# Forming the first quarter of a feed-forward hidden layer from seven block products instead of eight

## The chip, the cores and the metric

The kernel runs on one core of a Trainium2 chip. The metric is device time in microseconds (us) of one execution. Five engines work side by side, each through its own list of instructions in order: TensorE (PE, matrix products), VectorE (DVE), ScalarE (ACT), GpSimd (POOL) and SyncE (SP). In this kernel SP starts the plain loads from HBM, and POOL starts the loads that add what they bring to what already lies in the buffer ("accumulating loads").

## The reference, cut to what matters

One layer of a decoder trunk over 512 tokens with model width 1024. The part that is changed is the first product of the feed-forward step, and the part that reads it is the second:

```
h = rmsnorm(x, g_mlp[i])
x = x + jnp.square(jax.nn.relu(h @ w_ff1[i])) @ w_ff2[i]
```

Here `h` is 512 x 1024, `w_ff1` is 1024 x 4096 and `w_ff2` is 4096 x 1024. Before it come two attentions with their gates and the product with `w_o`; behind it comes a gated embedding (`w_pe`, `w_pg`) and a final norm. All is float32.

## The kernel before

Every product runs in float32r, a form in which TensorE takes a rounded operand. To keep float32 accuracy each operand is split in two: `hi`, rounded by ACT (line 75), and `lo = x - hi`, by DVE (line 76). `split` does both. Each product then takes three matmuls (`mm3`, lines 93 to 95): hi·hi, hi·lo and lo·hi. Weights come from HBM as units of 128 x 1024 numbers (512 KB).

Activations stand with the model dimension on the 128 partitions: `h2` is eight tiles (`h2_0` to `h2_7`) of 128 x 512 tokens, each as a pair hi and lo. They are made by `turned`: TensorE transposes the residual `x2` into a PSUM bank, and ACT and DVE split it from there with the gain as scale. The norm's factor is applied later (`rr`).

The feed-forward runs over four kilocolumns q (1024 of the 4096 hidden columns each). For each, eight blocks m of 128 columns are formed by `columns` (24 matmuls with 512 token columns each, PSUM tile `f{q}_{m}`), then relu and square give `u`. The second product over one kilocolumn, `products(q)`, already uses a scheme of seven block products for a 2 x 2 partition (Winograd's form): its steps are p1, p7, p6, p4, p5, p2, p3, with the PSUM tiles `pc`, `pb`, `pa`. Where such a product needs sums of weight blocks, the sum is formed in the buffer by accumulating loads (`more`, on POOL): the buffer `tx` is first loaded with one block and given a second (for p7), then a third (for p6), then a fourth (for p4). Each addition must wait until ACT and DVE have split the sum before it. `products` is a generator; the loop over q advances it between the blocks m of the next kilocolumn, so that TensorE alternates between the two.

The order of the instructions on each engine is fixed when the program is built, by a scheduler with a timeline of its own; on the chip each engine follows its list and waits wherever an operand isn't there. Buffers go round in pools: `fpool`'s tag `raw` has 8 buffers of 512 KB, and a load into a buffer waits for the last reader of what was there.

Of the kernel before, what the change touches and what calls it, by code (L numbers as in the profile page):

```python
# [11 lines left out]
F32 = mybir.dt.float32  # L12
# [28 lines left out]
def trunk(ctx, tc, xT_in, x_in, pT_in, w_in, w_up_a, w_up_b, w_o, w_ff1, w_ff2, w_pe, w_pg, g_final, pack, scratch, out):  # L41
# [119 lines left out]
    def gcol(i, k):  # L161
        return pk[:, 8 * i + k:8 * i + k + 1]
# [332 lines left out]
    def plain(name):  # L495
        return fpool.tile([P, U], F32, tag="raw", name=name, bufs=8)

    def factor(name):
        return [fpool.tile([P, U], F32R, tag=f"m{e}", name=f"m{e}{name}", bufs=2) for e in ("hi", "lo")]

# [27 lines left out]

    x2 = [[slot(f"x2_{t}{j}", "x") for j in range(2)] for t in range(NT)]

    def turned(name, dst, i, k, tag):
        ps = bank(f"{name}p{k}", tag)
        for t in range(NT):
            nc.tensor.transpose(ps[:, t * P:(t + 1) * P], x2[t][k // 4][:, k % 4 * P:(k % 4 + 1) * P], ident)
        split(*dst[k], ps, gcol(i, k))

    def squares(name, ss, j, t):
        nc.scalar.activation(half(f"{name}{j}{t}", "e", 3), x2[t][j], AF.Square, accum_out=ss[j][:, t:t + 1])


    h2 = [pair(f"h2_{k}", "h") for k in range(KD)]
    ss = [small(f"ss2_{j}", 4) for j in range(2)]
    for j in range(2):
        for t in range(NT):
            nc.sync.dma_start(x2[t][j], x_in[t * P:(t + 1) * P, j * S:(j + 1) * S])
        ps = [bank(f"wo{j}_{t}", (("p", "p", "p", "z"), ("at", "at", "o", "z"))[j][t]) for t in range(NT)]
        for c in range(4):
            whi, wlo = unit(w_o[4 * j + c], S)
            for k in range(2):
                hi, lo = merged[2 * c + k]  # L550
                for t in range(NT):
                    cols = slice(t * P, (t + 1) * P)
                    mm3(ps[t], hi[:, cols], lo[:, cols], whi[:, k], wlo[:, k], c == 0 and k == 0, c == 3 and k == 1)
            if j == 1 and c == 1:
                for k in range(4):
                    turned("h2", h2, 1, k, ("p", "p", "p", "z")[k])
        for t in range(NT):
            nc.vector.tensor_tensor(x2[t][j], x2[t][j], ps[t], op=ALU.add)
            squares("junk", ss, j, t)
    for _ in embed(0, ("p", "p", "p", "z")):  # L560
        pass
    for k in range(4, KD):
        turned("h2", h2, 1, k, ("at", "at", "o", "z")[k - 4])


    nc.vector.tensor_tensor(ss[0], ss[0], ss[1], op=ALU.add)
# [4 lines left out]

    tt = nc.vector.tensor_tensor

    def products(q, ua, ub):
        a11, a21 = [ua[:, :, i * 256:(i + 1) * 256] for i in range(2)]
        a12, a22 = [ub[:, :, i * 256:(i + 1) * 256] for i in range(2)]

        def load(name, kh, jh):  # L580
            t = [plain(f"{name}_{q}{c}") for c in range(2)]
            for c in range(2):
                nc.sync.dma_start(t[c], w_ff2[((q * 2 + kh) * 2 + jh) * 2 + c])
            return t

        def more(t, kh, jh):
            for c in range(2):
                nc.gpsimd.dma_start(t[c], w_ff2[((q * 2 + kh) * 2 + jh) * 2 + c], accum_op=ALU.add)  # L588

        def area(name, tag):  # L590
            return [bank(f"{name}{q}_{i}", tag) for i in range(2)]

        def product(name, a, b, ps, start=False, g=None, then=None):
            m = [x.rearrange("p (k c) -> p k c", k=4) for x in factor(f"{name}{q}")]
            w = []
            if not callable(a):
                split(*m, a, g)
            for c in range(2):
                count[0] += 1
                pool, n = ((wpool, 3), (fpool, 2))[c]  # L600
                w.append([pool.tile([P, U], F32R, tag=f"w{e}", name=f"w{e}{count[0]}", bufs=n) for e in ("hi", "lo")])
                split(*w[c], b[c])
            if callable(a):
                for h in range(2):
                    split(*[x[:, 2 * h:2 * h + 2] for x in m], a(h), g)
            for c in range(2):
                whi, wlo = [x.rearrange("p (k c) -> p k c", k=2) for x in w[c]]
# [12 lines left out]

        def mixed(name):
            return fpool.tile([P, U], F32, tag="s", name=f"{name}_{q}", bufs=2).rearrange("p (k c) -> p k c", k=4)

        def mix(name, x, y):
            s = mixed(name)
# [12 lines left out]
        ty = tx  # L638
        if q == 3:
            more(tx, 1, 0)  # L640
            ty = load("ty", 0, 1)
            more(ty, 1, 1)
            more(ty, 0, 0)
        t1, b21, b22 = load("t1", 0, 1), load("b21", 1, 0), load("b22", 1, 1)
        more(t1, 0, 0)
        yield
        ss = []

        def sums(h):
            if h == 0:  # L650
                ss.extend([mixed(f"s{i}") for i in (1, 2)])
# [12 lines left out]
        onto(pc, 1, 0)  # L664
        yield
        product("p5", s1, t1, pc, g=-1.0)
        onto(pb, 1, 0)
        yield
        pa = area("pa", "z")
        product("p2", a12, b21, pa, True)  # L670
        onto(pc, 1, 1)
        yield
        nc.vector.scalar_tensor_tensor(s2, a12, -1.0, s2, op0=ALU.mult, op1=ALU.subtract)

        def rest():
            onto(pa, 0, 0)
            if q == 3:
                first()

        product("p3", s2, b22, pc, then=rest)  # L680
        onto(pc, 0, 1)
        yield
# [8 lines left out]
                wg.append(unit(w_pg[k // 2], S))  # L691
            turned("h3", h3, 2, k, ("p", "p", "p", "o")[k])

    last = None
    for q in range(4):
        uu = [big(f"u{q}{i}", i, F32).rearrange("p (k c) -> p k c", k=4) for i in range(2)]
        this = products(q, *uu)
        for m in range(8):
            ps = bank(f"f{q}_{m}")
            columns(ps, unit(w_ff1[8 * q + m], P), h2)  # L700
            u = uu[m // 4][:, m % 4]
            nc.scalar.activation(u, ps, AF.Relu)
# [141 lines left out]
def _layout(x, p, w_in, w_up_a, w_up_b, w_o, w_ff1, w_ff2, w_pe, w_pg, g_mix, g_mlp, g_pe, g_final, sinks, rel_bias):  # L844
    pack = np.zeros((P, 168), np.float32)
    for i, g in enumerate((g_mix, g_mlp, g_pe)):
# [20 lines left out]
        "w_ff1": np.stack([_units(w_ff1, P * m, P) for m in range(DFF // P)]),  # L867
# [25 lines left out]
```

## Time and profile before

| | |
|---|---|
| median of 3 runs | 735.11 us (734.38 to 735.52) |
| the profiled execution | 733.58 us |
| its span, first to last instruction | 731.9 us |
| TensorE busy | 720.1 us, 98% of the span |
| VectorE, ScalarE busy | 501.2 us, 368.7 us |
| share of TensorE in the chain of work that ended last | 96% |

The span is what the profile's rows lie in; 1.7 us of the execution's own time lies around it. The rows give start times in us from the start of the span. A matmul's duration in the rows includes its way through the array (0.39 us for 512 columns), and the next one starts long before that has passed; what one costs is the distance between starts.

### The profile page before, as it was taken

To read this page: it belongs to the slowest core of one execution; us is meant where nothing else is said; L and a number is where in the kernel's file an instruction comes from. 1 tells how busy PE (TensorE), PEld (TensorE's weight loads), DVE (VectorE), ACT (ScalarE), POOL (GpSimd) and SP (SyncE) were. 2 spreads that over 40 slices of the span, in tenths; PEclk is the share of its full clock that TensorE was granted. 3 is DMA by queue.
4 is the path that set the end of the run, shared out by engine and by line. 5 is a ranking of instruction groups with operands and counts; after the bars stand their busy time and mean duration, and the time that the engine had idled before them with its cause. 6 is when DMAs were issued, how large, how long until landed. Compare 5 with 4: busy or idle time off the path is not lost.

```text
span 731.9 us, 9201 instructions
## 1 busy us (share of the span) xinstructions
PE 720.1 (98%) x3460; PEld 605.0 (83%) x3460; DVE 501.2 (68%) x731; ACT 368.7 (50%) x606; POOL 59.2 (8%) x84
## 2 busy tenths in 40 slices
PE   8999999999999999999999999999999999999995
PEld 7899888888888888888888888888888888888884
DVE  5695895898886548455275766666665765578586
ACT  7268978766544434345343433444434434245642
POOL 2010000211111000100000010101010011100000
PEclk9999999999999999999999999999999999999998
DMA  8331222122212225993235494647756589920202
GB/s 315 121 116 59 87 87 86 58 87 91 83 59 87 87 86 187 324 286 123 87 106 152 129 229 163 146 141 201 201 144 145 142 232 220 219 51 29 87 21 94
DMA packets 29227, 98.21 MB, mean 134 GB/s; under 512 B 3432, under 2 KB 3432, under 8 KB 29184
## 3 DMA queue, kind: packets, MB, share of 16 engines
q1 hardware_dynamic: 23040, 76.82, 30.5%
q0 software_dynamic: 5568, 20.01, 15.2%
q10 hardware_dynamic: 576, 0.80, 0.3%
q8 instruction: 27, 0.44, 0.2%
q14 instruction: 16, 0.13, 0.1%
HBM read 95.51 MB, written 2.11 MB: 133 GB/s over the span
## 4 chain that ended last, share of the span: by engine, by line
PE 96%; DVE 2%; ACT 1%; DMA 1%; issue 0%; SPq 0%; ACTq 0%
PE f L95 8%; PE f L94 8%; PE f L93 8%; PE pc L94 4%; PE pc L95 4%; PE pc L93 4%; PE bg L93 2%; PE bg L94 2%; PE ag L95 2%; PE bg L95 2%; PE ag L94 2%; PE ag L93 2%; PE wo L93 2%; PE wo L94 2%; PE pb L94 2%; PE pb L95 2%
## 5 line engine op out<-in xcount | busy, mean ns | idle before, releaser
L76 DVE TENSOR_TENSOR wlo<-wr,whi 128x1024 fp32r<-128x1024 f32 x86 | 105.1, 1223 | 78.8 <-ACT whi L75 78.3
L75 ACT CAST whi<-wr 128x1024 fp32r<-128x1024 f32 x86 | 90.2, 1052 | 135.7 <-PE f L94 30.5
L76 DVE TENSOR_TENSOR wlo<-b,whi 128x1024 fp32r<-128x1024 f32 x24 | 29.2, 1222 | 33.7 <-ACT whi L75 33.7
L94 PE MATMUL pc<-wlo,mhip 128*128 128x512 f32 x128 | 49.9, 390 | 0.0
L93 PE MATMUL pc<-whi,mhip 128*128 128x512 f32 x128 | 49.9, 390 | 0.0
L95 PE MATMUL pc<-whi,mlop 128*128 128x512 f32 x128 | 49.3, 389 | 0.0
L588 POOL DMA_DIRECT2D tx<-in_w_ff x24 | 20.8, 879 | 336.4 <-DVE wlo L76 162.6
L75 ACT CAST whi<-b 128x1024 fp32r<-128x1024 f32 x24 | 25.0, 1050 | 36.8 <-PE f L94 24.5
L76 DVE TENSOR_TENSOR wlo<-tx,whi 128x1024 fp32r<-128x1024 f32 x22 | 26.8, 1221 | 16.6 <-ACT whi L75 16.2
L75 ACT CAST whi<-tx 128x1024 fp32r<-128x1024 f32 x22 | 23.1, 1054 | 24.7 <-PE f L94 11.7
L413 DVE TENSOR_TENSOR_SCAN keep<-keep 128x128 f32<-128x128 f32 (+3 forms) x32 | 26.3, 860 | 3.8 <-POOL keep L408 1.9
L94 PEld LDWEIGHTS pc<-wlo,mhip 128*128 128x128 f32 x128 | 24.0, 188 | 5.2 <-DVE wlo L76 0.3
L93 PEld LDWEIGHTS pc<-whi,mhip 128*128 128x128 f32 x128 | 24.0, 188 | 5.0
L95 PEld LDWEIGHTS pc<-whi,mlop 128*128 128x128 f32 x128 | 24.0, 188 | 4.9
L75 ACT CAST mhip<-s 128x1024 fp32r<-128x1024 f32 (+1 forms) x16 | 13.4, 839 | 24.0 <-PE pc L94 12.8
L618 DVE SCALAR_TENSOR_TENSOR x<-pc,rr,x 128x512 f32<-128x512 f32 x32 | 22.6, 745 | 4.2 <-PE pc L95 4.2
L93 PE MATMUL wo<-whi,mg 128*128 128x512 f32 x64 | 25.0, 390 | 0.0
L94 PE MATMUL wo<-wlo,mg 128*128 128x512 f32 x64 | 24.9, 389 | 0.0
L93 PE MATMUL pb<-whi,mhip 128*128 128x512 f32 x64 | 24.9, 389 | 0.0
L94 PE MATMUL pb<-wlo,mhip 128*128 128x512 f32 x64 | 24.9, 389 | 0.0
L95 PE MATMUL pb<-whi,mlop 128*128 128x512 f32 x64 | 24.9, 389 | 0.0
L95 PE MATMUL wo<-whi,mg 128*128 128x512 f32 x64 | 24.7, 389 | 0.0
(987 smaller groups left out, 2122.6 us busy)
## 6 DMA issues: line engine op xcount, KB each, us to landing
wr<-in_w_in SPq DMA_DIRECT2D x32, 512.0 KB, 3.3
wr<-in_w_ff SPq DMA_DIRECT2D x32, 512.0 KB, 3.3
b<-in_w_ff SPq DMA_DIRECT2D x24, 512.0 KB, 4.6
tx<-in_w_ff POOLq DMA_DIRECT2D x24, 512.0 KB, 5.7
wr<-in_w_o SPq DMA_DIRECT2D x8, 512.0 KB, 3.9
tx<-in_w_ff SPq DMA_DIRECT2D x8, 512.0 KB, 3.2
t<-in_w_ff SPq DMA_DIRECT2D x8, 512.0 KB, 6.1
t<-in_w_ff POOLq DMA_DIRECT2D x8, 512.0 KB, 10.3
```

The costliest lines, as they stand in the source:

```text
L75: nc.scalar.copy(hi, src)
L76: nc.vector.tensor_tensor(lo, src, f32(hi), op=ALU.subtract)
L93: nc.tensor.matmul(ps, ahi, bhi, start=start, stop=False, skip_group_check=more)
L94: nc.tensor.matmul(ps, ahi, blo, start=False, stop=False, skip_group_check=more)
L95: nc.tensor.matmul(ps, alo, bhi, start=False, stop=stop, skip_group_check=more)
L413: nc.vector.tensor_tensor_scan(rev, rev, rev, 1.0, op0=ALU.mult, op1=ALU.min)
L588: nc.gpsimd.dma_start(t[c], w_ff2[((q * 2 + kh) * 2 + jh) * 2 + c], accum_op=ALU.add)
L618: nc.vector.scalar_tensor_tensor(x2[2 * i + t][j], ps[t], rr[j][:, 2 * i + t:2 * i + t + 1], x2[2 * i + t][j], op0=ALU.mult, op1=ALU.add)
```

## The change

The first kilocolumn (q = 0) of `h @ w_ff1` is no longer formed by eight `columns` blocks but by a new generator `hidden`, in seven block products over halves of the tokens (i), of the model rows (kh) and of the kilocolumn (jh). Each has four 128-column parts m, four 128-row parts k and 256 tokens: 48 matmuls with 256 columns. In the order of the program they are f1, f7, f6, f4, f5, f2, f3. They sum up in the PSUM tiles `fc` (f1, f6, f5, f3), `fb` (f7, f4) and `fa` (f2). `keep` copies a partial sum to `u`, `done` adds one to `u` and applies relu and square.

```diff
+    def blocks(src, q):
+        def load(name, kh, jh):
+            t = [plain(f"{name}_{q}{c}") for c in range(2)]
+            for c in range(2):
+                nc.sync.dma_start(t[c], block(c, kh, jh))
+            return t
+
+        def more(t, kh, jh):
+            for c in range(2):
+                nc.gpsimd.dma_start(t[c], block(c, kh, jh), accum_op=ALU.add)
...
-        split(*dst[k], ps, gcol(i, k))
+        if whole is None:
+            split(*dst[k], ps, gcol(i, k))
+        else:
+            nc.scalar.activation(whole, ps, AF.Copy, scale=gcol(i, k))
+            split(*dst[k], whole)
...
+    hf = [plain(f"hf{i}").rearrange("p (k c) -> p k c", k=2) for i in range(4)]
...
+            if j == 1 and c == 0:
+                f11, fx = fetch("f11", 0, 0), fetch("fx", 0, 1)
+                add(fx, 1, 1)
...
+    def hidden(ua, ub):
...
+        def product(name, a, b, ps, start=False, g=None):
+            w = halves(b)
+            if len(a) != 4:
+                m = [x.rearrange("p (k c) -> p k c", k=4) for x in factor(name)]
+                split(*m, a[0], g)
+                a = [[x[:, k] for x in m] for k in range(4)]
+            for m in range(4):
+                dst = ps[m // 2][:, m % 2 * 256:(m % 2 + 1) * 256]
+                for k in range(4):
+                    whi, wlo = [x[:, k % 2, m * P:(m + 1) * P] for x in w[k // 2]]
+                    mm3(dst, whi, wlo, *a[k], start and k == 0 and m % 2 == 0, k == 3, True)
...
+        chain, side = area("fc", "at"), area("fb", "z")
+        product("f1", known(0, 0), f11, chain, True)
+        s3 = mix(mixed("fs3"), rows(0, 0), rows(1, 0))
+        product("f7", [s3], fx, side, True)
+        keep(chain, 0, 0)
+        add(fx, 0, 0)
+        s1 = mix(mixed("fs1"), rows(1, 0), rows(1, 1))
+        s2 = mix(mixed("fs2"), s1, rows(0, 0))
+        f1 = fetch("f1", 0, 1)
+        add(f1, 0, 0)
+        yield
+        product("f6", [s2], fx, chain)
+        keep(side, 1, 1)
...
+        add(fx, 1, 0)
+        f21, f22 = fetch("f21", 1, 0), fetch("f22", 1, 1)
+        product("f4", known(1, 1), fx, side)
+        keep(chain, 1, 0)
+        product("f5", [s1], f1, chain, g=-1.0)
+        done(side, 1, 0)
+        yield
+        side = area("fa", "z")
+        product("f2", known(0, 1), f21, side, True)
+        done(chain, 1, 1)
+        product("f3", [s2], f22, chain)
+        done(side, 0, 0)
...
-    last = None
-    for q in range(4):
-        uu = [big(f"u{q}{i}", i, F32).rearrange("p (k c) -> p k c", k=4) for i in range(2)]
+    uu = kilo(0)
+    last = products(0, *uu)
+    sevens = hidden(*uu)
+    next(sevens)
+    next(sevens)
+    next(last)
+    next(sevens)
+    for q in range(1, 4):
+        uu = kilo(q)
         this = products(q, *uu)
...
-            if last and m < 5:
+            left = 8 - q
+            if m < left:
                 next(last)
-            if m in (3, 5, 6):
+            if m == left - 2:
+                next(this)
+            if left <= m < 7 + (q < 3):
                 next(this)
```

The unsplit `h2` is now kept in four buffers `hf` of the tag `raw`, since the sums s1, s2, s3 are made of it. The sums of weight blocks come from accumulating loads into `fx` (two halves, `fx_00` and `fx_01`: two blocks for f7, a third for f6, a fourth for f4) and into `f1` (two blocks, for f5).

On TensorE the rows behind the last transposes of `h2` were blocks `f0_m` with 512 columns. Before, they begin so:

```order
L534 MATMUL h2p7_3317<-ident_80,x2_31_2927 128x128
L93 MATMUL f0_0_3348<-h2_0h_2928,whi50_3351 128x512
L94 MATMUL f0_0_3348<-h2_0l_2929,whi50_3351 128x512
L95 MATMUL f0_0_3348<-h2_0h_2928,wlo50_3352 128x512
L93 MATMUL f0_0_3348<-h2_1h_2930,whi50_3351 128x512
```

Now the seven products stand there one behind the other, 336 matmuls, with no block of another kilocolumn between them. Where f6 ends (`fc1`, weights 55) and f4 begins (`fb0`, weights 56 and 57, the two halves of the last `fx`), the rows are:

```order
L95 MATMUL fc1_3371<-mhif6_3517,wlo55_3514 128x256
L93 MATMUL fb0_3372<-h2_4h_2936,whi56_3583 128x256
L94 MATMUL fb0_3372<-h2_4l_2937,whi56_3583 128x256
L95 MATMUL fb0_3372<-h2_4h_2936,wlo56_3584 128x256
L93 MATMUL fb0_3372<-h2_5h_2938,whi56_3583 128x256
L94 MATMUL fb0_3372<-h2_5l_2939,whi56_3583 128x256
L95 MATMUL fb0_3372<-h2_5h_2938,wlo56_3584 128x256
L93 MATMUL fb0_3372<-h2_6h_2940,whi57_3587 128x256
L94 MATMUL fb0_3372<-h2_6l_2941,whi57_3587 128x256
```

The seventh matmul of f4 is the first that needs `whi57`, the rounded second half of `fx` with its fourth block in it.

POOL's accumulating loads of the first kilocolumn were these before, all for `products(0)`:

```order
L588 DMA tx_00_3484<-in_w_ff2 128x1024
L588 DMA tx_01_3485<-in_w_ff2 128x1024
L588 DMA t1_00_3671<-in_w_ff2 128x1024
L588 DMA t1_01_3672<-in_w_ff2 128x1024
L588 DMA tx_01_3485<-in_w_ff2 128x1024
L588 DMA tx_00_3484<-in_w_ff2 128x1024
```

Now eight for `hidden` stand ahead of those (x2 is two equal rows in succession):

```order
L510 DMA fx_00_3132<-in_w_ff1 128x1024
L510 DMA fx_01_3133<-in_w_ff1 128x1024 x2
L510 DMA fx_00_3132<-in_w_ff1 128x1024 x2
L510 DMA f1_00_3503<-in_w_ff1 128x1024
L510 DMA f1_01_3504<-in_w_ff1 128x1024
L510 DMA fx_01_3133<-in_w_ff1 128x1024
L510 DMA tx_00_3709<-in_w_ff2 128x1024
```

So the last addition to `fx_01` stands behind the last one to `fx_00` and both of `f1`. SP's loads in the same stretch, which before were units of `w_ff1` in the order of m, are now:

```order
L87 DMA wr73_4090<-in_w_ff1 128x1024
L505 DMA f1_00_3503<-in_w_ff1 128x1024
L505 DMA f1_01_3504<-in_w_ff1 128x1024
L505 DMA f21_00_3575<-in_w_ff1 128x1024
L505 DMA f21_01_3576<-in_w_ff1 128x1024
L505 DMA f22_00_3579<-in_w_ff1 128x1024
L505 DMA f22_01_3580<-in_w_ff1 128x1024
L505 DMA b11_00_3705<-in_w_ff2 128x1024
```

The two of `f21` take over the buffers of `hf0` and `hf1`, which the sum s2 reads last; `f22_00` takes that of `fx_00` once it is split for f4, and `f22_01` and `b11_00` those of `hf2` and `hf3`.

## Rows read from the trace of the kernel before

**Rows 1.** The page: the chain that ended last, shares by engine

```profile
PE 96%; DVE 2%; ACT 1%; DMA 1%; issue 0%; SPq 0%; ACTq 0%
```

**Rows 2.** The longest waits of TensorE: for whom, us in total, times, longest

```profile
PE warm L150 <- DVE ones L144: 1.1, 1, 1.1
PE vb L93 <- ACT kvwhi L75: 1.1, 1, 1.1
...
```

**Rows 3.** TensorE in order of time, first kilocolumn: start, us, line; 20 rows

```profile
349.78 0.39 PE L95 MATMUL f<-h_4h,wlo 128*128 128x512 f32 x1
...
354.09 0.39 PE L94 MATMUL f<-h_7l,whi 128*128 128x512 f32 x1
```

**Rows 4.** The same with 256 columns, in the attention's values: 27 rows

```profile
42.88 0.28 PE L94 MATMUL va<-wlo,h_0h 128*128 128x256 f32 x1
...
45.99 0.28 PE L93 MATMUL va<-whi,h_1h 128*128 128x256 f32 x1
```

**Rows 5.** Busy us of PE, PEld, DVE, ACT, POOL; clock; DMA, by stretch

```profile
360.00:380.00 20.00, 20.00 (x90) 16.57 (x89) 12.02 (x13) 8.84 (x11) 0.85 (x1) 1.00 0.23 79
```

**Rows 6.** The turn from `w_o` to the first kilocolumn: DVE, then PE

```profile
337.30 1.23 DVE L76 TENSOR_TENSOR wlo<-wr,whi 128x1024 fp32r<-128x1024 f32 x1 [0.44 <-ACT whi L75]
344.32 0.74 DVE L79 SCALAR_TENSOR_TENSOR h_4l<-h2p,pk,h_4h 128x512 fp32r<-128x512 f32 x1
344.98 0.74 DVE L79 SCALAR_TENSOR_TENSOR h_5l<-h2p,pk,h_5h 128x512 fp32r<-128x512 f32 x1
...
341.41 1.91 PE L534 MATMUL h2p<-ident,x 128*128 128x128 f32 x16
343.08 0.47 PE L93 MATMUL f<-h_0h,whi 128*128 128x512 f32 x1
```

**Rows 7.** The page's costliest groups: the two halves of one split

```profile
L75 ACT CAST whi<-tx 128x1024 fp32r<-128x1024 f32 x22 | 23.1, 1054 | 24.7 <-PE f L94 11.7
L76 DVE TENSOR_TENSOR wlo<-tx,whi 128x1024 fp32r<-128x1024 f32 x22 | 26.8, 1221 | 16.6 <-ACT whi L75 16.2
```

**Rows 8.** From a finished split to the addition: DVE, then POOL

```profile
458.51 1.23 DVE L76 TENSOR_TENSOR wlo<-tx,whi 128x1024 fp32r<-128x1024 f32 x1 [3.08 <-ACT whi L75]
...
460.09 0.86 POOL L588 DMA_DIRECT2D tx<-in_w_ff  x1 [3.44 <-DVE wlo L76]
```

**Rows 9.** Three accumulating loads issued singly, 378.6 to 392.4: issue to landing

```profile
DMA to landing us min/median/max: 5.3/5.3/5.4
```

**Rows 10.** POOL in order of time, four accumulating loads close together

```profile
612.40 0.86 POOL L588 DMA_DIRECT2D ty<-in_w_ff  x1 [8.74 <-DMA ty<-in_w_ff]
612.99 2.05 POOL L588 DMA_DIRECT2D t<-in_w_ff  x2
618.99 0.86 POOL L588 DMA_DIRECT2D tx<-in_w_ff  x1 [3.95 <-DVE wlo L76]
```

**Rows 11.** Issue to landing of the fourth of them (618.99)

```profile
DMA to landing us min/median/max: 10.6/10.6/10.6
```

**Rows 12.** SP's plain loads around those four, and the landing of the later one

```profile
607.77 4.67 SPq L583 DMA_DIRECT2D b<-in_w_ff  x2
615.07 0.33 SPq L87 DMA_DIRECT2D wr<-in_w_pg  x1
...
DMA to landing us min/median/max: 9.8/9.8/9.8
```

**Rows 13.** The page: queues (q1 plain loads, q0 POOL's): packets, MB, share

```profile
q1 hardware_dynamic: 23040, 76.82, 30.5%
q0 software_dynamic: 5568, 20.01, 15.2%
```

**Rows 14.** TensorE's last matmul, and the stretches behind it (columns as rows 5)

```profile
722.49 0.28 PE L95 MATMUL pg<-wpg,h_7l 128*128 128x256 f32 x1
...
724.00:726.00 2.00, 0.00 (x0) 0.00 (x0) 1.83 (x9) 0.13 (x2) 0.00 (x0) 0.88 0.68 262
726.00:728.00 2.00, 0.00 (x0) 0.00 (x0) 1.71 (x6) 0.72 (x1) 0.00 (x0) 0.50 0.00 0
```

More of the change, by code (lines that the diff above doesn't have):

```diff
@@ L496, in plain, with block, halves, mixed @@
         return fpool.tile([P, U], F32, tag="raw", name=name, bufs=8)
+    def blocks(src, q):
+        def block(c, kh, jh):
+            return src[((q * 2 + kh) * 2 + jh) * 2 + c]
+        def load(name, kh, jh):
[6 more added lines that the diff above has]
+                nc.gpsimd.dma_start(t[c], block(c, kh, jh), accum_op=ALU.add)
+        return load, more
+    def halves(b):
+        w = []
+        for c in range(2):
+            count[0] += 1
+            pool, n = ((wpool, 3), (fpool, 2))[c]
+            w.append([pool.tile([P, U], F32R, tag=f"w{e}", name=f"w{e}{count[0]}", bufs=n) for e in ("hi", "lo")])
+            split(*w[c], b[c])
+        return [[x.rearrange("p (k c) -> p k c", k=2) for x in y] for y in w]
+    def mixed(name):
+        return fpool.tile([P, U], F32, tag="s", name=name, bufs=2).rearrange("p (k c) -> p k c", k=4)
     def factor(name):
@@ L529, in trunk, with turned @@
     x2 = [[slot(f"x2_{t}{j}", "x") for j in range(2)] for t in range(NT)]
-    def turned(name, dst, i, k, tag):
+    def turned(name, dst, i, k, tag, whole=None):
         ps = bank(f"{name}p{k}", tag)
@@ L541, in trunk @@
     h2 = [pair(f"h2_{k}", "h") for k in range(KD)]
+    hf = [plain(f"hf{i}").rearrange("p (k c) -> p k c", k=2) for i in range(4)]
     ss = [small(f"ss2_{j}", 4) for j in range(2)]
+    tt = nc.vector.tensor_tensor
+    fetch, add = blocks(w_ff1, 0)
     for j in range(2):
@@ L553, in trunk @@
                     mm3(ps[t], hi[:, cols], lo[:, cols], whi[:, k], wlo[:, k], c == 0 and k == 0, c == 3 and k == 1)
+            if j == 1 and c == 0:
+                f11, fx = fetch("f11", 0, 0), fetch("fx", 0, 1)
+                add(fx, 1, 1)
             if j == 1 and c == 1:
                 for k in range(4):
-                    turned("h2", h2, 1, k, ("p", "p", "p", "z")[k])
+                    turned("h2", h2, 1, k, ("p", "p", "p", "z")[k], hf[k // 2][:, k % 2])
         for t in range(NT):
@@ L562, in trunk @@
     for k in range(4, KD):
-        turned("h2", h2, 1, k, ("at", "at", "o", "z")[k - 4])
+        turned("h2", h2, 1, k, ("o", "p", "p", "p")[k - 4], hf[k // 2][:, k % 2])
     nc.vector.tensor_tensor(ss[0], ss[0], ss[1], op=ALU.add)
@@ L570, in trunk, with rows, known, area @@
     nc.vector.tensor_scalar(rr[1], rr[0], -1.0, None, op0=ALU.mult)
-    tt = nc.vector.tensor_tensor
+    def hidden(ua, ub):
+        u = [[x[:, :, i * 256:(i + 1) * 256] for x in (ua, ub)] for i in range(2)]
+        def rows(i, kh):
+            return [hf[2 * kh + c][:, :, i * 256:(i + 1) * 256] for c in range(2)]
+        def known(i, kh):
+            return [[x[:, i * 256:(i + 1) * 256] for x in h2[4 * kh + k]] for k in range(4)]
+        def area(name, tag):
+            return [bank(f"{name}{i}", tag) for i in range(2)]
+        def product(name, a, b, ps, start=False, g=None):
[9 more added lines that the diff above has]
+                    mm3(dst, whi, wlo, *a[k], start and k == 0 and m % 2 == 0, k == 3, True)
+        def mix(s, x, y):
+            for c in range(2):
+                xc, yc = [z[c] if isinstance(z, list) else z[:, 2 * c:2 * c + 2] for z in (x, y)]
+                tt(s[:, 2 * c:2 * c + 2], xc, yc, op=ALU.subtract)
+            return s
+        def parts(ps, i, j):
+            return [(u[i][j][:, 2 * b:2 * b + 2], ps[b].rearrange("p (m c) -> p m c", m=2)) for b in range(2)]
+        def keep(ps, i, j):
+            for dst, src in parts(ps, i, j):
+                nc.scalar.copy(dst, src)
+        def done(ps, i, j):
+            for dst, src in parts(ps, i, j):
+                tt(dst, dst, src, op=ALU.add)
+            full = u[i][j]
+            nc.scalar.activation(full, full, AF.Relu, scale=(1.0, -1.0)[j])
+            nc.scalar.activation(full, full, AF.Square)
+        chain, side = area("fc", "at"), area("fb", "z")
[11 more added lines that the diff above has]
+        keep(side, 1, 1)
+        for c in range(2):
+            nc.vector.scalar_tensor_tensor(s2[:, 2 * c:2 * c + 2], rows(0, 1)[c], -1.0, s2[:, 2 * c:2 * c + 2],
+                                           op0=ALU.mult, op1=ALU.subtract)
+        add(fx, 1, 0)
[10 more added lines that the diff above has]
+        done(side, 0, 0)
+        for dst, src in parts(chain, 0, 1):
+            nc.scalar.activation(dst, src, AF.Relu, scale=-1.0)
+        nc.scalar.activation(u[0][1], u[0][1], AF.Square)
+        yield
@@ L578, in products @@
         a12, a22 = [ub[:, :, i * 256:(i + 1) * 256] for i in range(2)]
[L580 to L588, printed above, removed]
+        load, more = blocks(w_ff2, q)
         def area(name, tag):
@@ L594, in product @@
             m = [x.rearrange("p (k c) -> p k c", k=4) for x in factor(f"{name}{q}")]
-            w = []
             if not callable(a):
                 split(*m, a, g)
[L598 to L602, printed above, removed]
+            w = halves(b)
             if callable(a):
@@ L606, in product @@
             for c in range(2):
-                whi, wlo = [x.rearrange("p (k c) -> p k c", k=2) for x in w[c]]
+                whi, wlo = w[c]
                 for k in range(2):
@@ L619, in onto @@
                                                x2[2 * i + t][j], op0=ALU.mult, op1=ALU.add)
-        def mixed(name):
-            return fpool.tile([P, U], F32, tag="s", name=f"{name}_{q}", bufs=2).rearrange("p (k c) -> p k c", k=4)
         def mix(name, x, y):
-            s = mixed(name)
+            s = mixed(f"{name}_{q}")
             tt(s, x, y, op=ALU.subtract)
@@ L650, in sums @@
             if h == 0:
-                ss.extend([mixed(f"s{i}") for i in (1, 2)])
+                ss.extend([mixed(f"s{i}_{q}") for i in (1, 2)])
             ks = slice(2 * h, 2 * h + 2)
@@ L692, in first, with kilo @@
             turned("h3", h3, 2, k, ("p", "p", "p", "o")[k])
-    last = None
-    for q in range(4):
-        uu = [big(f"u{q}{i}", i, F32).rearrange("p (k c) -> p k c", k=4) for i in range(2)]
+    def kilo(q):
+        return [big(f"u{q}{i}", i, F32).rearrange("p (k c) -> p k c", k=4) for i in range(2)]
+    uu = kilo(0)
[7 more added lines that the diff above has]
+        uu = kilo(q)
         this = products(q, *uu)
@@ L866, in _layout @@
         "w_o": np.stack([_units(w_o, S * j, S, 2 * c, 2) for j in range(2) for c in range(4)]),
-        "w_ff1": np.stack([_units(w_ff1, P * m, P) for m in range(DFF // P)]),
+        "w_ff1": np.stack([_units(w_ff1, S * j, S, 4 * k + 2 * c, 2) for k in range(2) for j in range(2) for c in range(2)]
+                          + [_units(w_ff1, P * m, P) for m in range(8, DFF // P)]),
         "w_ff2": np.stack([_units(w_ff2, S * j, S, 8 * q + 4 * k + 2 * c, 2)
```

## The prediction

> **What bounds the kernel now.** I read the chain of work that ended last first: TensorE holds 96% of it [rows 1]. Then TensorE's waits: the two longest are 1.1 us each and lie at the start of the program [rows 2]. So TensorE is the bound, and in the first kilocolumn nothing else shows: in the stretch 360 to 380 it is busy for all 20 us at full clock, while DVE is busy for 12.02 and ACT for 8.84 [rows 5]. There a change gains what it takes off TensorE, as long as it leaves no new hole in TensorE's row. Both are to be worked out.
>
> **What the change takes off TensorE.** Before, the first kilocolumn is 8 blocks of 24 matmuls with 512 columns, 192 in all. From 349.78 to 354.09 lie 19 distances between starts: 4.31 / 19 = 0.2268 us each [rows 3]. Now it is 7 products of 48 matmuls with 256 columns, 336. Matmuls of that shape stand in the values of the attention: 42.88 to 45.99, 26 distances, 3.11 / 26 = 0.1196 us [rows 4]; the weights are 128 x 128 there as here, so that their loading is hidden as well as it will be here. 192 x 0.2268 = 43.5 us against 336 x 0.1196 = 40.2 us: **-3.4 us**. The columns fall by an eighth, the time only by 7.7%, because a short matmul costs a little more than half a long one. The 16 transposes stay.
>
> **What it adds on ACT and DVE.** DVE gets in the 40 us of the seven products, counted from its order, 14 subtractions of 128 x 1024 (1.22 us each [rows 7]) and 16 of half that size (0.66 us apart, 344.32 to 344.98 [rows 6]): 17.1 + 10.6 = 27.7 us of 40. ACT gets less, since its cast is 1.05 us [rows 7], with one more short pass for each tile of `h2` (`hf`). Neither becomes the bound, and I cost their work at nothing by itself; TensorE's matmuls cover it, 5.7 us a product (48 x 0.1196). What counts is the chain through `fx`.
>
> **The chain through fx.** In the list of TensorE f1, f7, f6 and f4 follow each other without a filler; f7, f6 and f4 all use the one buffer `fx`, and between two uses lie a split, an addition from HBM and a split. I lay it out.
> - The last transposes start at 341.41 and the first matmul behind them at 343.08 [rows 6]; ahead of that point TensorE has the same work in both kernels. Without a wait f1, f7 and f6 take 144 matmuls, and the seventh of f4, the first to need `whi57`, would start at 343.08 + 150 x 0.1196 = 361.0.
> - `wlo52`, the split of `fx_00` for f7, stands in DVE's list where a weight's split stands before, behind the last sums with `w_o`: it ends at 337.30 + 1.23 = 338.5 [rows 6]. From such an end to the addition's issue are 460.09 - 459.74 = 0.35 us [rows 8]: 338.9. The loads that are free by then were issued long before, so this one runs alone: 5.3 us [rows 9], landed at 344.2. ACT 1.05 and DVE 1.22 [rows 7], and 0.1 for hand-over: split by 346.6. f6 is due at 343.08 + 96 x 0.1196 = 354.6; until then DVE has eight half-size steps (the sums s1 and s2, the lo parts of `h2`) and two splits left for it, 8 x 0.66 + 2 x 1.22 = 7.7 us, to 354.3: it just fits, no wait.
> - At 346.95 POOL issues the third addition to `fx_00`, and behind it, about 1 us apart, the two for `f1`. The third addition to `fx_01` must wait for `wlo55`, in DVE's list behind eight half-size steps: 346.6 + 8 x 0.66 + 1.22 + 0.35 = 353.4. So four accumulating loads leave POOL at about 0, 1, 2 and 6.5 us.
> - Alone the last one would land at 353.4 + 5.3 = 358.7, in time. But the trace has this very pattern: 612.40, 612.99 (two), 618.99 [rows 10], that is 0 to 2.6 and 6.6 us, and there the fourth lands 10.6 us after its issue, at 629.6 [rows 11]. The work explains it. On the page POOL's queue takes 15.2% of 731.9 us for 20.01 MB, 2.9 us of all 16 engines for 0.52 MB, and a plain load 1.5 us (30.5%, 76.82 MB) [rows 13]: four additions are 11.6 us, and the two plain loads in that stretch (612.1 and 615.07 [rows 12]) 3.0 us.
> - Here the plain loads in the same window are `f21_00`, `f21_01`, `f22_00`, `f22_01`, `b11_00`: five. How many get through before the fourth addition is not known. The load of 615.07 needed 9.8 us beside the additions [rows 12], so plain loads are held up as well. Lower bound, none: 346.95 + 5.3 + 3 x 2.9 = 361.0. Upper, all five: 353.4 + 10.6 + 3 x 1.5 = 368.5. I take three, one more than in the row: 353.4 + 10.6 + 1.5 = **365.5**.
> - `whi57` is cast at 365.5 + 0.1 + 1.05 = 366.7. TensorE stands from 361.0 to 366.7: **+5.7 us** (+1.2 and +8.7 at the bounds). Behind the waiting matmul stand the rest of f4, then f5, f2, f3: all of them shift, and nothing gives it back, since DVE, ACT and the loads of `f21` and `f22` were waiting on the same transfers. `wlo57` comes 1.22 us later, after eleven matmuls that don't need it (1.3 us).
>
> On such a queue the Trainium skill ("DMA: Bandwidth & Descriptors", Queues, rings and completion order) says that each DMA engine takes turns between the queues it has work for. By that rule all five plain loads would be served while the additions wait, and the sum would be its upper bound. The 9.8 us of [rows 12] agree with taking turns only in part, as more additions than loads went through.
>
> **The clock.** Five us without a matmul are new in this kernel's middle. At the end of the program the last matmul starts at 722.49, the granted clock is 0.88 as a mean of 724 to 726 and 0.50 after it [rows 14], that is 1.2 GHz: it fell some 3 us behind the last matmul. So I expect it to fall in the hole. What the return costs no row shows: nothing at the least, and at the most f4's remaining 42 matmuls at twice 0.1196, 5.0 us. I take a third, **+1.5 us**, since the return is likely done within f4.
>
> **Behind it.** In the second product p1 needs `u`, ready after f2, and f3 and one block of 5.4 us (24 x 0.2268) stand between. From q = 0 to 2 only one block stands between p7 and p6 (two before): 2 x 5.4 = 10.9 us from start to start, against 0.35 + 5.3 + 0.1 + 1.05 + 1.22 = 8.0 for addition and split; p6 to p4 has just that distance before and waits for nothing [rows 2]. I cost both at nothing; if that cover were gone, 8.0 us less what lies between would show as a wait of `pc`. The tail of the program is the same list.
>
> **Sum.** -3.4 + 5.7 + 1.5 = **+3.8 us**: 733.6 becomes 737.4 for the profiled execution. The median of the runs lies 1.5 us higher (735.11), so the predicted time is **738.9 us**.
>
> **The rivals.**
> - *The additions don't hold each other up*, `fx_01` lands by 359.9 (361.0 - 1.1) and the full gain stays: 735.1 - 3.4 = 731.7. For it speaks that an addition alone takes 5.3 us [rows 9], which would do; against it the 10.6 us of [rows 11]. It decides at a landing of 359.9, 13 us behind the first of four additions, which is nearly what they take without a plain load. Chance of this and of a gain over 0.2%: 0.19. The Trainium skill ("DMA: Bandwidth & Descriptors", Anatomy of one DMA) gives such a load about 2.0 us and the bytes at 436 GB/s, an estimate of 3.2 us for 0.52 MB; by that rule this rival would hold with time to spare. The trace disagrees: 5.3 us at the least.
> - *The hole eats just the gain.* The landing is 361.7 to 364.7, as at two plain loads or fewer: -3.4 + 2 to 5 us, and the clock hardly falls. 735 us, within 0.2% (1.5 us, about what a measurement of this kernel can tell from no change). Chance 0.18.
> - *f6 waits too.* If the second addition to `fx_00` lands not after 5.3 but, as beside other traffic, after up to 10.6 us [rows 11], the split ends 5.3 us later, f6 starts some 5 us late and the next additions move by as much: up to 743. For it speaks that f6 just fits; against it that SP has nothing to load just then. Chance 0.08.
> - *DVE becomes the bound*: 27.7 of 40 us, no; 0.02, some 740.
>
> **Chances and range.** The forecast itself (738.9, its own range 736.6 to 742.5) gets 0.53. Slower by over 0.2% is this and the last two: 0.63. The range reaches down to the lower bound of the transfers (735.1 - 3.4 + 1.2 = 732.9, and a little of the measurement's spread), up to five loads with a third of the clock's bound (735.1 - 3.4 + 8.7 + 1.5 = 741.9): **732.4 to 742.3**; the full gain without a hole and a late f6 stay outside.
>
> **What would show it.** In the profile after: distances of 0.1196 us in `fc`, `fb`, `fa`; a wait of TensorE for ACT's cast of `fx` (`fb<-h_6h,whi`), 3 to 8 us, and no other new one over 1 us; behind it a stretch with a granted clock of 0.5; four landings on POOL's queue of 5 to 12 us. Wrong it would be if POOL's last addition to `fx` lands within 6 us of its issue, if TensorE's hole stands at f6, or if the short matmuls start further apart than 0.12 us because their weights can't be loaded in time.

## The result and the profile after

The changed kernel takes 738.86 us (median of 5 runs, 737.24 to 741.25), the kernel before 735.11 us: a ratio of 1.0060, with a 95% interval of 1.0044 to 1.0076 (a ratio is formed from all runs and can differ by 0.1% from that of the medians). It is slower by 0.6%, and the forecast was 738.9 us. The profiled execution took 737.24 us and its span is 735.5 us, against 731.9 us before.

From the page of the changed kernel, POOL's DMA queue (packets, MB, share of 16 engines) and the shares of the chain that ended last:

```profile
q0 software_dynamic: 6720, 24.21, 18.9%
...
PE 91%; DVE 3%; DMA 3%; ACT 1%; issue 0%; SPq 0%; ACTq 0%
```

TensorE's share of the chain falls from 96% [rows 1] to 91%, and the 3% of DMA (22 us) say that the chain now runs through transfers somewhere. POOL's queue takes 18.9% of 735.5 us for 46 loads of 0.52 MB (24.21 MB), 3.0 us each of all 16 engines, about as before (2.9 [rows 13]). The waits of TensorE (whom it waited for, us in total, times, longest) say where:

```profile
PE fb L93 <- ACT whi L75: 4.5, 1, 4.5
PE vb L93 <- ACT kvwhi L75: 1.4, 1, 1.4
```

One new wait stands above those of [rows 2], of the product f4 (`fb`) for ACT's cast of a weight. TensorE's rows in order of time around it, with the first rows of f7, f6 and f4 ahead:

```profile
349.20 0.28 PE L93 MATMUL fb<-mhif,whi 128*128 128x256 f32 x1
...
354.96 0.40 PE L93 MATMUL fc<-mhif,whi 128*128 128x256 f32 x2
...
360.72 0.28 PE L93 MATMUL fb<-h_4h,whi 128*128 128x256 f32 x1
...
361.32 0.28 PE L95 MATMUL fb<-h_5h,wlo 128*128 128x256 f32 x1
366.11 0.58 PE L93 MATMUL fb<-h_6h,whi 128*128 128x256 f32 x1 [4.52 <-ACT whi L75]
366.49 0.42 PE L94 MATMUL fb<-h_6l,whi 128*128 128x256 f32 x1
...
370.55 0.31 PE L95 MATMUL fb<-h_5h,wlo 128*128 128x256 f32 x1
```

Three things stand here. From 349.20 to 360.72 are f7 and f6, 96 matmuls in 11.52 us, 0.1200 us each, so the short matmuls cost what [rows 4] said. The seventh matmul of f4 was due at 361.32 + 0.12 = 361.44 and starts at 366.11, a hole of 4.67 us. Behind it, from 366.49 to 370.55, lie 19 distances in 4.06 us, 0.214 each; at 0.12 they would be 2.28, so this stretch loses 1.8 us, and with the first, slow distance (0.38 for 0.12) 2.0 us. The busy times by stretch (PE, PEld, DVE, ACT, POOL, then TensorE's granted clock, the DMA share and GB/s), which answer to [rows 5], name the reason:

```profile
360.00:365.00 5.00, 1.59 (x14) 1.39 (x12) 0.85 (x1) 0.00 (x0) 0.00 (x0) 0.88 1.03 311
365.00:370.00 5.00, 3.89 (x18) 3.89 (x19) 3.69 (x4) 4.85 (x6) 0.00 (x0) 0.50 0.85 327
```

The granted clock falls within the hole and is 0.50 (1.2 GHz) from 365 to 370. DVE and ACT are nearly idle in the hole (0.85 us and nothing in 360 to 365): they wait as well. Only the DMA engines are full. POOL's issues in order of time:

```profile
339.15 0.86 POOL L510 DMA_DIRECT2D fx<-in_w_ff  x1 [21.41 <-DVE ss L605]
347.34 0.85 POOL L510 DMA_DIRECT2D fx<-in_w_ff  x1 [7.33 <-DVE wlo L76]
348.01 1.95 POOL L510 DMA_DIRECT2D f<-in_w_ff  x2
353.30 0.86 POOL L510 DMA_DIRECT2D fx<-in_w_ff  x1 [3.35 <-DVE wlo L76]
```

ACT's row with the cast that ends TensorE's wait, and that waits for the transfer itself:

```profile
365.02 1.04 ACT L75 CAST whi<-fx 128x1024 fp32r<-128x1024 f32 x1 [5.43 <-DMA fx<-in_w_ff]
```

The DMA view of the stretch lists the issues (tile, engine, count, KB each, median us from issue to landing); the first row is that of 347.34, the second the two for `f1`, the third that of 353.30:

```profile
fx<-in_w_ff POOLq DMA_DIRECT2D x1, 512.0 KB, 5.2
f<-in_w_ff POOLq DMA_DIRECT2D x2, 512.0 KB, 10.8
...
fx<-in_w_ff POOLq DMA_DIRECT2D x1, 512.0 KB, 11.7
```

The last addition lands 11.7 us after its issue, at 365.0, where that of 347.34, with no other addition ahead of it, needs 5.2.

From the issue of 347.34 to that landing at 365.02 the DMA view has for the two queues (packets, MB, share of 16 engines):

```profile
q0 software_dynamic: 576, 2.10, 64.2%
q1 hardware_dynamic: 551, 2.05, 30.7%
```

In these 17.7 us POOL's queue moved just the four additions (2.10 MB are 4 x 0.52) in 11.3 us of all engines, and the plain loads 2.05 MB, as much as 3.9 of them, in 5.4 us. Together that is 95% of the stretch: the engines were at work for nearly all the time that the addition was on its way.

The account of the two spans: -3.2 us for the columns (336 x 0.1200 = 40.3 for 43.5), +4.7 the hole, +2.0 the clock, +0.3 the longer wait of `vb` at the start of the program, and -0.1 behind TensorE's last matmul (9.2 us from its start at 726.26 to the end of the span, 9.4 before [rows 14]). Together +3.7 us with these rounded terms, and 735.5 - 731.9 is 3.6.

### The profile page after: what moved, and what is told of

Same layout as the page of the kernel before. It is cut to its first block, busy times and chain, and to the rows that moved or that the text cites. A ratio compares the mean times of both kernels' runs of the same rounds, so it can differ in the third digit from the quotient of the medians.

```text
span 735.5 us, 9559 instructions
## 1 busy us (share of the span) xinstructions
PE 719.1 (98%) x3604; PEld 611.3 (83%) x3604; DVE 514.5 (70%) x747; ACT 388.2 (53%) x631; POOL 66.1 (9%) x92
## 3 DMA queue, kind: packets, MB, share of 16 engines
q0 software_dynamic: 6720, 24.21, 18.9%
## 4 chain that ended last, share of the span: by engine, by line
PE 91%; DVE 3%; DMA 3%; ACT 1%; issue 0%; SPq 0%; ACTq 0%
PE f L94 6%; PE f L93 6%; PE f L95 6%; PE pc L94 4%; PE pc L93 4%; PE pc L95 4%; DMA fx<-in_w_ff 2%; PE bg L93 2%; PE bg L94 2%; PE ag L95 2%; PE bg L95 2%; PE ag L94 2%; PE ag L93 2%; PE pb L93 2%; PE pb L94 2%; PE pb L95 2%
## 5 line engine op out<-in xcount | busy, mean ns | idle before, releaser
L75 ACT CAST whi<-wr 128x1024 fp32r<-128x1024 f32 x78 | 81.7, 1051 | 101.9 <-PE ag L94 18.2
L76 DVE TENSOR_TENSOR wlo<-wr,whi 128x1024 fp32r<-128x1024 f32 x78 | 95.2, 1221 | 42.9 <-ACT whi L75 42.5
L76 DVE TENSOR_TENSOR wlo<-b,whi 128x1024 fp32r<-128x1024 f32 x24 | 29.0, 1221 | 27.7 <-ACT whi L75 27.7
```

## The experiments

All ratios are to the kernel before, run beside each experiment on the same chip. The theory under test: the addition is late because the additions issued ahead of it on POOL's queue are served first, and because plain loads come between; its delay is TensorE's hole; and the hole makes the clock fall. The rivals are that only the plain loads hold it up, that additions in flight share the engines, and that the slow stretch behind the hole is not the clock's.

### The last addition ahead of the two for f1

```diff
         f1 = fetch("f1", 0, 1)
-        add(f1, 0, 0)
         yield
         product("f6", [s2], fx, chain)
...
         add(fx, 1, 0)
+        add(f1, 0, 0)
...
+    with tc.manual_schedule(engines={mybir.EngineType.Pool}):
```

The last line pins POOL's list to the order of the program, since the scheduler otherwise puts the issues back as they were; the third block is added to `fx_01` ahead of `fx_00`, as in the changed kernel.

> The third addition to fx_01 is issued ahead of the two for f1; nothing else changes on POOL. Theory (an addition lands late because those issued before it on POOL's queue are served first): it goes out at about 353.3 as now, but with nothing in front of it, lands within 5 to 6 us (358.6 to 359.3), whi57 is cast by 360.4, f4 doesn't wait, the clock doesn't fall: 738.9 - 4.7 - 2.0 = 732.2 us, up to 0.6 more if f5 now waits for f1. Rival 1 (the plain loads of the window hold the addition up, not its own queue): it still takes about 11 us, 738.9. Rival 2 (the additions overtake each other or share): landing at 361 to 363, a hole of 1 to 3 us, 733 to 736.

Measured: 734.69 us, ratio 1.0002 (0.9989 to 1.0015). POOL's issues in this kernel, that of the last addition to `fx_01` and those of the two for `f1`:

```profile
352.77 0.85 POOL L510 DMA_DIRECT2D fx<-in_w_ff  x1 [5.20 <-DVE wlo L76]
353.33 2.06 POOL L510 DMA_DIRECT2D f<-in_w_ff  x2
```

Their landings:

```profile
fx<-in_w_ff POOLq DMA_DIRECT2D x1, 512.0 KB, 6.8
f<-in_w_ff POOLq DMA_DIRECT2D x2, 512.0 KB, 11.9
```

The same addition, issued at the same point with the same plain loads issued around it, lands after 6.8 us instead of 11.7, and f4 waits no longer for its cast (0.5 us are left, for `wlo57`). So the additions ahead of it are worth 4.9 us, and the plain loads alone don't make it late. But the time is not the expected one. The delay has gone to whoever is last now: TensorE's rows in f5 (`fc`):

```profile
367.28 0.28 PE L95 MATMUL fc<-mhif,wlo 128*128 128x256 f32 x1
368.64 0.39 PE L93 MATMUL fc<-mhif,whi 128*128 128x256 f32 x1 [1.08 <-ACT whi L75]
368.87 0.28 PE L94 MATMUL fc<-mlof,whi 128*128 128x256 f32 x1
369.90 0.38 PE L95 MATMUL fc<-mhif,wlo 128*128 128x256 f32 x1 [0.75 <-DVE wlo L76]
...
370.77 0.42 PE L95 MATMUL fc<-mhif,wlo 128*128 128x256 f32 x1
370.98 0.42 PE L93 MATMUL fc<-mhif,whi 128*128 128x256 f32 x1
```

The two for `f1` now need 11.9 us on average, and f5 waits for the second of them: two holes, 1.24 and 0.91 us beyond a matmul's distance of 0.12 (367.28 to 368.64, 368.87 to 369.90). Behind them the matmuls of 256 columns take 0.42 and start 0.21 us apart: the clock fell here too. The expectation allowed for 0.6 us in f5 and no fall, and there the miss in the time lies. Of the queue it said 5 to 6 us with nothing in front; the 6.8 us are more than that, and the plain loads, of which 0.78 MB moved meanwhile, are what is left to explain the rest.

### The two additions for f1 early

```diff
-        add(fx, 0, 0)
+        add(fx, 0, 0, (1, 0))
+        f1 = fetch("f1", 0, 1)
+        add(f1, 0, 0)
         s1 = mix(mixed("fs1"), rows(1, 0), rows(1, 1))
...
-        f1 = fetch("f1", 0, 1)
-        add(f1, 0, 0)
...
+    with tc.manual_schedule(engines={mybir.EngineType.Pool}):
```

> The two additions to f1 are issued right behind the second addition to fx_00 (339.2), so that they are through before the third additions go out. Theory (first come, first served, some 3 us of the engines each): fx_00 lands at 344.6 as now, the two for f1 by 348 and 351, the third to fx_00 by 353.5, the third to fx_01, issued at 353.3, by 359.3: no hole in f4, no fall of the clock, 732.2 us. Rival (additions in flight share the engines): the second to fx_00 is slowed by the two behind it and lands at 347 to 350, f6, due at 355 and with its operands ready just before that now, waits 2 to 5 us and everything behind shifts: 734 to 738. If only the third matters and sharing is the rule, the time is above 733 in any case.

Measured: 731.46 us, ratio 0.9957 (0.9941 to 0.9973), which beats both kernels. The longest wait of TensorE in this kernel is one of 1.1 us at the start of the program.

POOL's issues:

```profile
340.46 0.86 POOL L510 DMA_DIRECT2D fx<-in_w_ff  x1 [19.53 <-DVE ss L605]
341.02 2.06 POOL L510 DMA_DIRECT2D f<-in_w_ff  x2
348.52 0.85 POOL L510 DMA_DIRECT2D fx<-in_w_ff  x1 [5.45 <-DVE wlo L76]
354.47 0.86 POOL L510 DMA_DIRECT2D fx<-in_w_ff  x1 [5.09 <-DVE wlo L76]
```

Their landings in the same order:

```profile
fx<-in_w_ff POOLq DMA_DIRECT2D x1, 512.0 KB, 5.4
f<-in_w_ff POOLq DMA_DIRECT2D x2, 512.0 KB, 9.1
fx<-in_w_ff POOLq DMA_DIRECT2D x1, 512.0 KB, 7.5
fx<-in_w_ff POOLq DMA_DIRECT2D x1, 512.0 KB, 7.0
```

The busy times and the clock over the 40 us of the seven products:

```profile
342.00:382.00 40.00, 40.00 (x333) 39.75 (x332) 27.95 (x32) 29.54 (x38) 6.26 (x8) 1.00 0.99 252
```

The addition with two others right behind it lands after 5.4 us, like one alone: what comes later on the queue doesn't slow what is ahead, and the rival of shared engines falls. The last addition needs 7.0 us. TensorE is busy for all 40 us at full clock; the median is 3.4 us below the 734.86 of the kernel before, and by the ratio it is 3.2. So the gain of the columns is there, with nothing lost again.

### Without the two additions for f1

```diff
         f1 = fetch("f1", 0, 1)
-        add(f1, 0, 0)
```

> The two additions to f1 are left out (f5 then uses one weight block instead of a sum of two, all else is computed). Theory (the addition to fx_01 is late because of the additions ahead of it on POOL's queue): it lands 6 to 7.5 us after its issue at 353.3, as the one issued with nothing ahead of it did (6.8), by 360.8; whi57 by 361.9 against 361.4 due: a hole of 0 to 0.5 us, no fall of the clock, 732.2 to 732.7. Rival (the plain loads do it): 10 us or more, 737 to 739.

Measured: 731.56 us, ratio 0.9962 (0.9950 to 0.9975). POOL's last addition to `fx_01` and, from ACT's rows, the cast that waits for it:

```profile
356.07 0.85 POOL L510 DMA_DIRECT2D fx<-in_w_ff  x1 [5.21 <-DVE wlo L76]
```

```profile
362.85 1.05 ACT L75 CAST whi<-fx 128x1024 fp32r<-128x1024 f32 x1 [3.17 <-DMA fx<-in_w_ff]
```

It lands 6.8 us after its issue by the DMA view, although all plain loads are issued where they were, and the view of TensorE's waits names none but those at the start of the program. All these rows lie 2.9 us later than in the changed kernel, and so does the first matmul of f1 (344.94 for 342.07): that comes from the start of the program, of which more below. Taking the two additions away from in front gives the same as issuing them early.

### The plain loads behind the additions

```diff
-        f21, f22 = fetch("f21", 1, 0), fetch("f22", 1, 1)
         product("f4", known(1, 1), fx, side)
         keep(chain, 1, 0)
         product("f5", [s1], f1, chain, g=-1.0)
+        f21, f22 = fetch("f21", 1, 0, fx), fetch("f22", 1, 1, f1)
...
+    with tc.manual_schedule(engines={mybir.EngineType.SP}):
```

The last argument of `fetch` is the buffer to load into, so that SP, in the order of the program, waits until `fx` and `f1` are split.

> f21 and f22 are loaded into the buffers of fx and f1 once these are split, so that of the five plain loads in the window of the additions only one (f21_00, from about 355.4) is left, and the loads for the second product come behind it. Theory with both parts (additions 2.9 us each, one behind another, plain loads 1.5 us each between them): fx_01 lands at 361.3 without and 362.8 with that one load, hole in f4 1.0 to 2.5 us, hardly a fall of the clock: 738.9 - 4.7 - 2.0 + 1.0 to 2.5 = 733.2 to 734.7 us. Rival 1 (only the additions count): landing at 365, 738.9. Rival 2 (only the plain loads count): landing by 359, no hole, 732.2.

Measured: 735.95 us (732.31 to 737.93), ratio 1.0015 (1.0000 to 1.0030). The profiled execution took 732.31 us, the least of all, so that its trace doesn't explain the median. Two more executions of the same kernel were profiled.

> The kernel with the late plain loads a second time, for a second trace: its profiled execution took 732.3 us with holes of 1.7 and 0.9 us and a granted clock of 1.00, its median of ten 736.0. Theory (a hole of that length lets the clock fall in some executions and not in others): in an execution of 735 us or more the same holes stand in the trace, with a stretch at a granted clock of 0.5 behind them. Rival (the transfers themselves take different times): the holes are 4 us or longer in such an execution, and the clock is of no account.

> The same once more, with the same expectation: a time near 732 with the clock at 1.00 behind the holes, a time of 735 or more with a stretch at 0.5, and holes of about 1.7 and 0.9 us in both.

They took 735.41 and 736.34 us. TensorE's rows behind the sixth matmul of f4 in the first trace:

```profile
362.49 0.39 PE L93 MATMUL fb<-h_6h,whi 128*128 128x256 f32 x1 [1.38 <-ACT whi L75]
...
364.09 0.28 PE L94 MATMUL fb<-h_7l,whi 128*128 128x256 f32 x1
```

In the second:

```profile
364.54 0.39 PE L93 MATMUL fb<-h_6h,whi 128*128 128x256 f32 x1 [1.80 <-ACT whi L75]
...
366.39 0.41 PE L94 MATMUL fb<-h_7l,whi 128*128 128x256 f32 x1
```

In the third:

```profile
365.16 0.39 PE L93 MATMUL fb<-h_6h,whi 128*128 128x256 f32 x1 [2.49 <-ACT whi L75]
...
367.01 0.41 PE L94 MATMUL fb<-h_7l,whi 128*128 128x256 f32 x1
```

The same matmul takes 0.28 us in the first trace and 0.41 in the others: the clock stayed at 1.00 in the one and fell to 0.50 in the other two. The landings are 8.6, 9.2 and 9.7 us after the issue, the waits 1.38, 1.80 and 2.49 us (a second hole, which the expectations put at 0.9 us, is one of 0.7 from start to start). So the two expectations on the spread both hold in part: the transfers differ by 1.1 us between executions, and the slow matmuls (some 14 distances of 0.21 where 0.12 is usual) add some 1.4.

Neither expectation saw the largest part of the difference, which lies far ahead of the additions. The first matmul of f1 in the first and in the second trace:

```profile
341.58 0.36 PE L93 MATMUL fc<-h_0h,whi 128*128 128x256 f32 x1
```

```profile
343.22 0.36 PE L93 MATMUL fc<-h_0h,whi 128*128 128x256 f32 x1
```

In the third it starts at 343.14. Some 1.6 of the 3.1 and 4.0 us by which the second and the third execution are longer lie ahead of it, at the start of the program: there the matmuls of 512 columns start 0.43 us apart for a few us in the second and the third trace (8.24 to 8.67, 8.26 to 8.69), in the first 0.23 (7.30 to 7.53). The kernels without a hole have this spread too: the first matmul of f1 starts at 343.37 with the early additions and at 344.94 without the two.

For the transfers the theory with both parts is the one that is left: one plain load in the window in place of five (0.51 MB there in the first trace) makes 11.7 us into 8.6 to 9.7, not into 7 or less, and not into 11.7. The landings agree: in the changed kernel those of the four additions come 4.5, 4.2 and 3.8 us apart (352.6, 357.0, 361.2 and 365.0 by the DMA view), in the first trace here, with nothing between the first three, 2.5, 2.5 and 4.2 (352.2, 354.6, 357.2 and 361.4).

### TensorE kept busy in the hole

```diff
                 for k in range(4):
+                    if busy and m == 0 and k == 2:
+                        ps0 = bank("busy")
+                        for n in range(busy):
+                            tc.keep_in_program_order(nc.tensor.matmul(ps0, h2[0][0][:, :P], h2[0][0], start=n == 0, stop=n == busy - 1))
...
-        product("f4", known(1, 1), fx, side)
+        product("f4", known(1, 1), fx, side, busy=20)
```

> 20 more matmuls of 512 columns, whose result nobody reads, stand in TensorE's row ahead of the one that waits for whi57: 20 x 0.2268 = 4.5 us of work in the hole of 4.7 us. Theory (the 2 us behind the hole are the clock's): the wait shrinks to 0.2 us, the granted clock stays at 1.00, the rest of f4 runs at 0.12 us a matmul: 738.9 - 2.0 = 736.9 us. Rival (the slow stretch behind the hole has another cause, as late operands): 738.9 and the distances of 0.213 us stay.

Measured: 737.07 us, ratio 1.0039 (1.0023 to 1.0055), against 1.0060 for the changed kernel. TensorE's rows from the extra matmuls on:

```profile
363.67 2.43 PE L636 MATMUL busy<-h_0h 128*128 128x512 f32 x10
366.09 0.39 PE L93 MATMUL fb<-h_6h,whi 128*128 128x256 f32 x1
...
369.24 0.28 PE L95 MATMUL fb<-h_7h,wlo 128*128 128x256 f32 x1
369.36 0.28 PE L93 MATMUL fb<-h_4h,whi 128*128 128x256 f32 x1
```

The matmul that needs `whi57` starts as late as in the changed kernel (366.09 for 366.11), but the rest of f4 runs at 0.12 us a matmul. The granted clock is 1.00 there (from 360 to 365 and from 365 to 370). The slow stretch is the clock's. The two ratios have intervals that overlap, so the times alone don't show a gain; the traces do. Their f1 starts at the same time (342.00 for 342.07), and the span is 1.0 us shorter (734.5 for 735.5), with useless work of 4.5 us on TensorE. That is half of the 2.0 us, since the list behind the wait is ordered otherwise here and a wait of 0.8 us for `wlo57` comes back.

### Useful work in the hole

```diff
         add(fx, 1, 0)
         f21, f22 = fetch("f21", 1, 0), fetch("f22", 1, 1)
+        yield
...
     next(sevens)
+    ahead = kilo(1)
+    column(1, 0, ahead)
     next(sevens)
```

`column(1, 0, ahead)` is the body of the loop over m for the first block of the second kilocolumn, which the loop then leaves out; the steps of `products(0)` follow one block later.

> The additions stay in the order of the changed kernel; the first block of the second kilocolumn (24 matmuls of 512 columns, 5.4 us, and one more plain load in the window for its successor) is formed between f7 and f4, so that f4 starts at 366.2 instead of 360.7. Theory (the loss is only TensorE standing still, and the clock's fall that follows from it): whi of the late fx_01 is ready at 366.1 as now, up to 1.5 later for the one more load, and is needed at 366.9: hole 0 to 0.7 us, no fall of the clock, 732.2 to 733.0 us. Rival (the block is missing later as a cover, between the products of the second product): a new wait of up to 3 us in front of one of p1 to p4, 734 to 736.

Measured: 731.90 us, ratio 0.9967 (0.9956 to 0.9978). TensorE's rows at the late half:

```profile
366.65 0.32 PE L93 MATMUL fb<-h_6h,whi 128*128 128x256 f32 x1
367.84 0.39 PE L95 MATMUL fb<-h_6h,wlo 128*128 128x256 f32 x1 [0.76 <-DVE wlo L76]
```

The addition is as late as ever (11.5 us by the DMA view) and costs one wait of 0.8 us in place of the hole and the slow stretch, 6.7. No wait appears later; the rival of a missing cover falls.

## Why the prediction was right

**The columns.** 0.1196 us a matmul was taken from [rows 4], 0.1200 was measured; -3.4 us was forecast, and by the measured distance it is -3.2; the kernel with the early additions shows it whole (a ratio of 0.9957, 731.46 against 734.86).

**DVE and ACT.** 27.7 of 40 us were counted for DVE; from 342 to 382 in the kernel with the early additions, whose seven products go without a hole from 343.4 to 385, it is busy for 27.95.

**The chain through fx.** Its points were 338.9, 346.95 and 353.4 for the additions; they were issued at 339.15, 347.34 and 353.30. f6 was to fit just so: its last operand (`mlof6`) was forecast for 354.3 and f6 started at 354.96 without a wait.

**The landing.** Forecast 365.5, measured 365.0. The sum was 10.6 us from [rows 11] and 1.5 for one more plain load. The experiments support both halves of it: with nothing ahead on the queue the addition takes 6.8 us (7.0 and 6.8 in two other kernels), and with one plain load in the window in place of five it takes 8.6 to 9.7. The number of three plain loads was a choice between none and five, one more than the two that were counted around the four additions of [rows 10]. The DMA view of the kernel before, from 612.40 to 629.60, has more for the plain loads there than two:

```profile
q1 hardware_dynamic: 446, 1.59, 27.8%
```

1.59 MB are as much as three loads, and in the changed kernel it was 3.9. So both counts were too low by one, and the difference, which is all that the sum uses, was right. The lower bound of 2.9 us for each addition behind the first is seen best where the loads are out of the way: from 346.77 to 361.3 (352.73 + 8.6) are 14.5 us, against 5.3 + 3 x 2.9 = 14.0.

**The hole.** Forecast 5.7, measured 4.67: the landing was 0.5 us early, and TensorE's due time 0.4 us later than 361.0 (0.3 of it from the start of the program).

**The clock.** Forecast 1.5 us as a third of a bound, measured 2.0; filling the hole took the fall away. This term was the least founded, and that it came out so near is luck: in the kernel with late loads, with shorter holes, the fall comes in two executions and stays away in one.

**Behind it** nothing was given back and no wait was added, as forecast, and the median lies 1.6 us above the profiled execution (1.5 taken). The sum came out at +3.6 us by -3.2, +4.7 and +2.0 where -3.4, +5.7 and +1.5 had been put, so an error of 1.0 us is partly cancelled by those of 0.2 and 0.5, and the start of the program adds 0.3. The mechanism was foreseen; that the median agrees to less than 0.1 us is luck, as the five runs lie 4.0 us apart.

**The rivals.** That additions don't hold each other up is refuted by the first and the third experiment, where the last one lands after 6.8 us once the two for `f1` are out of its way. The estimate of 3.2 us that the Trainium skill ("DMA: Bandwidth & Descriptors", Anatomy of one DMA) gives for such a transfer is disagreed with by every addition here, 5.2 us at the least. A hole that just eats the gain was nearer than its chance of 0.18 says: its landing ended at 364.7, 0.3 us ahead of the measured one, and the kernel with late loads is that case. f6 did not wait, and DVE is not the bound.

The rule that each DMA engine takes turns between the queues (the Trainium skill, "DMA: Bandwidth & Descriptors", Queues, rings and completion order) agrees with what the plain loads cost, 1.4 us where no addition is ahead (6.8 against 5.4), and with the landings, some 4 us apart with plain loads between the additions and 2.5 without. The prediction took from it that all five loads would be served ahead of the last addition; the 3.9 that were are nearer to one load for each addition. The same section says, of the queues that SP and ACT issue on, that each DMA engine takes the work of a ring in order, though a later write may end first; it doesn't say so of POOL's. Here POOL's queue went in order: an addition with two behind it took 5.4 us.

## What to carry to other kernels

In these kernels accumulating loads on one queue were served in the order of issue, some 3 us of all DMA engines each for 512 KB; so the list of the issuing engine is a schedule, and a sum that is needed last is issued early, while the queue is empty, not in front of the one that is needed next. Saving on TensorE is worth only what the chain of sums behind it can follow: before a scheme with fewer products is laid out back to back, lay out its transfers, or put a block of other work where the chain is longest. A hole in TensorE's row can cost more than its length, by the clock, and other work in it can give that part back. Before two traces are compared, see where the first difference lies: here up to 3.5 us of it lay at the start of the program (f1 starts at 341.48 in one kernel's trace and at 344.94 in another's), far from the change.

## What the runs showed of the hardware

- The granted clock fell to 0.50 behind holes far shorter than the one at the end of the program [rows 14]: holes of 1.4 and 1.0 us from start to start in the first experiment, of 2.1 us (362.47 to 364.54) in the second trace with late loads; behind 1.7 and 0.7 us in the first trace it stayed at 1.00. In the third trace TensorE was at work again when it fell: behind the hole the matmuls from 365.38 to 365.73 start 0.12 us apart, those from 366.80 on 0.21. The ten times of this kernel lie 5.6 us apart, those of the kernel before, of the one with the early additions, of the one without the two and of the one with useful work in the hole 2.7 to 3.9; f1 starts anywhere from 341.5 to 344.9 in the single traces, so the start of the program can make much of either.
- The slow stretch behind a hole cost 2.0 us in the changed kernel, where the matmuls ran at 0.214 us from 366.5 to 370.5, and some 1.4 in the second and third trace with late loads, behind holes of 2.1 and 2.8 us. The Trainium skill ("TensorE: Matmul & The Clock Gate", Part 1: The HAM clock gate) says of the start of a kernel that the number of slow matmuls differs from run to run; the three traces of the kernel with late loads agree for its start, and show the same for a place in its middle: none in one, 3 us of them in two.
- An addition is not slowed by additions that are issued after it (5.4 and 5.2 us with two behind it, 5.3 alone [rows 9]).
